# Reordering first operands, projection steps, a mask and one tile split in an encoder layer

## The chip, the cores and the metric

The kernel runs on one core of a Trainium2 chip. The metric is the device time in microseconds (us) of one execution. Time before: 967.51 us, the median of three runs (967.51, 967.21 and 969.06).

The engines have short names here, as in the profile: PE is TensorE (matmuls), DVE is VectorE, ACT is ScalarE, POOL is GpSimd, SP is SyncE, which issues nearly all DMAs of this kernel. Each engine executes its own instructions in the order of the program; between engines they wait on semaphores.

## The reference

One encoder layer is applied to 256 prompt tokens and to 2048 sample tokens, all in float32, with a width of 1024:

```
h = rms_norm(x, g_pre)
q, k, v, z_a, u_f, z_f = split(h @ w_in)               # w_in is 1024 x 3072
y_a = neighbourhood_attention(q, k, v, rpb)            # 8 heads of 64, 64-column grid,
                                                       # 8 rows x 16 columns window, bias, softmax
y_f = real(fft2(u_f, over tokens and within a group)) @ w_f + b_f
mixed = [rms_norm(y_a, g_na) * silu(z_a), rms_norm(y_f, g_f) * silu(z_f)]
out = x + rms_norm(mixed @ w_out, g_post)
```

## The kernel before

**Numbers.** Every float32 matrix product is done as three matmuls in a reduced format (`mm3`, L159 to L162: high by high, low by high, high by low). For this each operand x is split: `h` is a copy of x on ACT, rounded to the format, and `l = x - h` is a subtraction, mostly on DVE. So a split is a pair of an ACT instruction and a DVE instruction behind it, and PE needs `h` first and `l` one matmul later.

**Stages, in order of time.** (1) Projections v and u of the prompt and the other four prompt projections: the loop `for b in range(16)`, up to about 119 us. (2) `vu(0, ...)`, v and u of the sample's second product family, 14 groups of 12 matmuls, 119 to 158 us. (3) The projection steps `for i in range(16)` with seven groups `j` each, with `vu(1, ...)` between steps 7 and 8, up to about 530 us. (4) The Fourier stages. (5) The attention loop `for k in range(2, 37)`, four head pairs `pr` of nine groups `i` each, with the Fourier half of the output product `f_mm` between. (6) The dense run, the attention half of the output product `a_mm`, from about 869 us.

The order of the instructions is the program's: everything is written out by hand, and an operation stands in its engine's queue where its function is called. Buffers are taken from pools in turn, and the writer of a new tile waits until the readers of the tile that had the buffer are done. The pool `k8` holds tiles of 8 KB per partition: the tokens `nx` and their combinations, the splits `xh`, `xl` of them, and the rows `xm` whose squares are summed for the norm.

**Functions that the change touches.**
- `op_split(j)` (L466) splits operand j of `vu`: per half `vh` on ACT (L477) and `vl` on DVE (L478); for j = 5 in other forms (L473, L474). `op_load` issues the loads (L463).
- `n_first(j)` (L425) makes the token operand j of `vu(0)`: `xh` on ACT (L428) and `xl` on DVE (L429), both from `k8`.
- `rows_load(i)` (L288) loads 256 rows into a tile `xm` of `k8`; `rows_square(i)` (L292) squares them on ACT (L295) with a sum.
- `hooks` and `at(i, ...)`: functions called ahead of the i-th group of `vu`. In `vu(0)` a hook is called behind the `op_load` and `op_split` of the same group. The order of groups is j = 0, 0, 1, 1, 2, 2, 3, 3, 4, 4, 5, 5, 6, 6; the evictions (L505) of a group follow its matmuls.
- `w_load`, `w_sums`, `a_split`: load of the weights of a projection step (L232 by `load`), four POOL sums (L532), and the splits `wa` (ACT L546, DVE L547). They are called one or two steps ahead.
- `u_load`, `u_split` (ACT L367, DVE L368), `u_stage1` (two pairs of matmuls `pz`, copy `z` on ACT L375, store to `ZD`): the first Fourier stage on 16 tiles `ut`, strewn between the groups of the steps 9 to 14.
- `n_load`, `n_scale` (DVE L400), `n_diff` (POOL, with stores `n_put`): the tokens of the second pass, in steps 1 to 4.
- `mask_p(pr)` (POOL L1114): subtracts the prompt's mask from a bias table; `bias_max` (DVE L1207) of the next head pair's first group reads it. `soft` divides the softmax on POOL (L1219).
- `ys_split(d)` (ACT L1440, DVE L1445): splits a tile of the output product; `atiles[1]` is the second one of the dense run. `pv` multiplies probabilities and v (L1543) and finishes a tile of attention (`y`, L1557; `sqa`, L1563).

Of the kernel before, what the change touches and what calls it, by code (L numbers as in the profile page):

```python
# [164 lines left out]
def build(tc, A, O):  # L165
# [590 lines left out]
    for b in range(16):  # L756
        kind, blk = divmod(b, 4)
        if 1 <= b < 10:
            wz_load(1)
        if b == 2:  # L760
            n_load((1, 1))
        if b in (5, 7):
            r_put(b // 2 + 1)
        if b == 10:
            op_load(0)
        if b == 12:
            op_load(1)
        if 2 <= b < 14:
            b_raw(b + 2)
        if 2 <= b < 8:  # L770
            x, y = divmod(b, 2)
            n_scale(None, *divmod(x, 2)[::-1], range(2 * y, 2 * y + 2))
        elif 8 <= b < 12:
            n_sum(b - 8)
        if b in (5, 12, 13):
            n_first((5, 12, 13).index(b) + 1)
        if b > 13:
            op_split(b - 14)
        p = mmt(512)[:, :TP]
        wh, wl = wb.pop(b)  # L780
        for k in range(KC):
            mm3(nc, p, wh[:, k], wl[:, k], hp_[:, k], lp_[:, k], k == 0, k == KC - 1)
        o = st.tile([128, 256], F32, tag="f", name="f", bufs=3)
        if kind % 2:
            i, d = p, o
        else:
            i = p.rearrange("p (b r c) -> p b r c", b=2, c=32)
            d = o.rearrange("p (r b c) -> p b r c", b=2, c=32)
        nc.scalar.activation(d, i, AF.Silu if kind < 2 else AF.Copy)
        if kind < 2:  # L790
            nc.sync.dma_start(zD[kind, blk * 128:blk * 128 + 128, :TP], o)
        else:
            nc.sync.dma_start((kD if kind == 2 else qD)[blk, :, :TP], o)
# [15 lines left out]
        hooks.setdefault(i, []).append(call(f, *a))  # L809

    for x in range(4, 7):
        at(3 * x - 12, n_first, x)
    for x in range(4):
        at(2 * x + 1, rows_load, x + 5)
        at(2 * x + 4, rows_square, x + 5)
# [19 lines left out]
    for i in range(16):  # L835
        sg, pr = divmod(i, 8)
        if i == 8:
            hooks.clear()
            for x in (5, 6):
                at(2 * x - 9, b_split, x)  # L840
            for x in range(4):
                if x:
                    at(4 * x, wo_load, x)
                at(4 * x + 5, wo_split, x)
            at(20, w_load, 8)
            at(24, w_sums, 8)
            for j in range(7):
                at(24 + j // 2, a_split, 8, j)
            vu(1, range(4), hooks)
        kind, blk = divmod(2 * pair(i), 4)  # L850
        o = [st.tile([128, 1024], F32, tag="f", name="f", bufs=3) for x in range(2)]
        uu = {}

        def e_(name):
            uu[name] = st.tile([128, 512], F32, tag="e", name=name, bufs=6)
            return uu[name]

        def dst(f, b):
            if kind % 2 == 0:
                return o[f].rearrange("p (x b c) -> p b x c", b=2, c=32)[:, b]  # L860
            if kind == 1:
                return o[f].rearrange("p (a b j) -> p b a j", b=2, j=256)[:, b]
            return o[f].rearrange("p (y b x c) -> p y x b c", y=2, b=2, c=16)[:, b]

        def src(a):
            if kind % 2 == 0:
                return a.rearrange("p (x c) -> p x c", c=32)
            if kind == 1:
                return a.rearrange("p (a j) -> p a j", j=256)
            return a.rearrange("p (x b c) -> p x b c", b=2, c=16)  # L870

        def comb(f, b, u, p, op=ALU.add):
            nc.vector.tensor_tensor(out=dst(f, b), in0=src(uu[u]), in1=src(p), op=op)  # L873

        def store(f):
            ts = slice(TP + 1024 * sg, TP + 1024 * sg + 1024)
            if kind < 2:
                silu_[0] = nc.scalar.activation(o[f], o[f], AF.Silu)
                nc.sync.dma_start(zD[kind, (blk + f) * 128:(blk + f) * 128 + 128, ts], o[f])
            else:  # L880
                nc.sync.dma_start((kD if kind == 2 else qD)[blk + f, :, ts], o[f])

        silu_ = [None]
        for j in range(7):
            if i in (0, 8):
                if j in (0, 3):
                    w_load(i + 1 + j // 3)
                if i == 0 and j == 0:
                    a_split(0, 6)
                if i == 0 and j == 1:  # L890
                    row_scales(10, 8)
                if i == 0 and j == 4:
                    iv_rows(10, 8)
                    iv_put(10, 8)
                if i == 0 and j == 6:
                    iv_get(10, 8)
                if j == 2:
                    w_sums(i + 1)
                for x in {3: (0, 1), 4: (2, 3), 5: (4, 5), 6: (6,)}.get(j, ()):
                    a_split(i + 1, x)  # L900
            elif i not in (7, 15):
                if j == 0:
                    w_sums(i + 1)
                a_split(i + 1, j)
                if j == 3 and i < 14 and i != 6:
                    w_load(i + 2)
            elif i == 7:
                if j in (3, 4):
                    op_load(j - 3)
                if j in (5, 6):  # L910
                    op_split(j - 5)
                if j == 5:
                    wo_load(0)
            if sg == 0:
                x, y = divmod(7 * (pr - 1) + j, 14)
                if x in (0, 1):
                    if y == 0:
                        n_load(x)
                    elif 3 <= y < 7:
                        n_scale(x, *divmod(y - 3, 2))  # L920
                    elif 7 <= y < 12:
                        n_diff(x, y - 7)
                if pr == 6 and j in (2, 5):
                    (b_split if j > 2 else b_get)(0)
                if pr == 7 and j:
                    b_get(j)
                    if j > 2:
                        b_split(j - 2)
            if i == 2 and j == 0:
                for t, n in ((gmix, "gmix"), (bfs, "bf"), (dnyq, "dnyq"), (rmask, "rmask"), (csm, "csmask")):  # L930
                    nc.sync.dma_start(t, A[n])
                nc.sync.dma_start(cm, A["cmask"].rearrange("p (b x) -> p b x", b=2))
            for f, d in ((u_load, 0), (u_split, 4), (u_stage1, 6)):
                x = 7 * pr + j - 7 - d
                if sg and 0 <= x < 38 and x % 7 in (2, 4, 6):
                    f(x // 7 * 3 + x % 7 // 2 - 1)
            if i == 5 or 8 <= i < 15:
                t_step(max(0, i - 7), j)
            if i == 15 and j in (1, 3, 4, 5):
                if j == 1:  # L940
                    d2 = [load_d(0), load_d(1)]
                else:
                    zgs.append(load_z(j - 3))
            if 9 <= i < 15 and j == 2:
                v_copy(i - 9)
            p = mmt(512)
            aw = aop[i, j]
            bh, bl = bnew[sg, j]
            for k in range(4):
                mm3(nc, p, aw[:, 0, k], aw[:, 1, k], bh[:, k], bl[:, k], k == 0, k == 3)  # L950
            add = lambda o, u: nc.vector.tensor_tensor(out=e_(o), in0=uu[u], in1=p, op=ALU.add)
            if j == 0:
                nc.scalar.copy(e_("u0"), p)
            elif j == 1:
                comb(0, 0, "u0", p)
            elif j == 2:
                add("u2", "u0")
            elif j == 3:
                add("u4", "u2")
            elif j == 4:  # L960
                comb(1, 1, "u4", p)
                add("u3", "u2")
            elif j == 5:
                comb(1, 0, "u3", p, ALU.subtract)
                store(1)
            else:
                comb(0, 1, "u4", p)
                store(0)
        if kind < 2:
            silu = silu_[0]  # L970
# [624 lines left out]
    for k in range(2, len(G) + 1):  # L1595
# [48 lines left out]
        if g:  # L1644
            if k + 1 < len(G):
                split_q(G[k + 1])
            soft(g, 1)
            if k == 2:
                ys_mul(ftiles[x])
# [6 lines left out]
            f_mm(k, range(6, 12))  # L1656
        else:
            a_mm(atiles[0], 1, range(6))
        if pr < 3 and i == 8:
            mask_p(pr + 1)  # L1660
        if k % 2 and x < 18:
            ys_split(ftiles[x])
        if pr < 3 and i in (5, 6, 7, 8):
# [2 lines left out]
            ys_split(atiles[0])  # L1666
        if g:
            f_evac(k)
        if f:
            pv(f)  # L1670
        if k + 1 in NT:
# [15 lines left out]
        if k in (34, 35):  # L1687
            ys_load(atiles[k - 33])
            of_load(atiles[k - 34])
        if k == 36:  # L1690
            ys_split(atiles[1])


    def evac(d, p, ns, q):
# [110 lines left out]
```

## Time and profile before

| | |
|---|---|
| Median of three runs | 967.51 us (967.21 to 969.06) |
| The profiled execution | 968.71 us, of which 966.9 us are the span |
| PE busy | 957.0 us, 99% |
| DVE, ACT, POOL busy | 710.4, 496.2, 429.8 us |
| Granted PE clock, mean | 0.997 |
| DMA moved | 269.81 MB, mean 279 GB/s |

How to read the lines below: a row of the timeline has the start in us from the span's start, the duration in us, the engine, the line of the kernel, the operation, output<-input by tile names, the shapes (partitions x elements), the count (several rows on end of one kind are put together) and in brackets the idle time of the engine before it with what ended that. The waits view has engine, instruction, releaser, then total us, times, longest. The profiled execution is 1.2 us above the median of the runs.

### The profile page before, as it was taken

The page shows a single profiled execution, that of the slowest core. Times are in us where ns is not written, and L with a number is a line of the kernel's source. Part 1 is how long each engine was busy: PE and PEld are TensorE (multiplying, and loading weights), DVE is VectorE, ACT ScalarE, POOL GpSimd, SP SyncE. Part 2 cuts the span into 40 slices and gives each one's busy share as a digit, 9 for nine tenths or more (in the row PEclk, how much of TensorE's full clock was granted, in tenths as well). Part 3 has the DMA queues.
Part 4 walks back from the last instruction along what each step waited for, and adds up shares of the span by engine and source line. Part 5 has one row for each costly group of instructions (what it writes and reads, how often), then busy time and mean ns, then how long its engine had stood idle before and what let it go on. Part 6 is the DMA issues. An engine that isn't in the chain of part 4 may idle for free.

```text
span 966.9 us, 16988 instructions
## 1 busy us (share of the span) xinstructions
PE 957.0 (99%) x5743; PEld 798.7 (83%) x5743; DVE 710.4 (73%) x1310; ACT 496.2 (51%) x1077; POOL 429.8 (44%) x400
## 2 busy tenths in 40 slices
PE   9999999999999999999999999999999999999997
PEld 8889988888888888888887889787787887778886
DVE  6758978687886855798887358776666656649997
ACT  5845676423335432233344267676676766644443
POOL 2200002455752202665655044567677786524544
PEclk9999999999999999999999999999999999999998
DMA  8899696557748893599888895698877998979993
GB/s 304 323 359 374 243 347 244 194 189 276 292 189 358 293 352 117 193 386 335 294 308 319 292 346 208 197 278 280 267 234 245 273 312 260 281 255 333 342 341 130
DMA packets 140942, 269.81 MB, mean 279 GB/s; under 512 B 13402, under 2 KB 81840, under 8 KB 137464
## 3 DMA queue, kind: packets, MB, share of 16 engines
q1 hardware_dynamic: 140360, 268.32, 79.9%
q8 instruction: 46, 0.75, 0.3%
q10 hardware_dynamic: 432, 0.39, 0.1%
q14 instruction: 40, 0.33, 0.1%
q0 software_dynamic: 64, 0.02, 0.0%
HBM read 179.00 MB, written 96.81 MB: 285 GB/s over the span
## 4 chain that ended last, share of the span: by engine, by line
PE 92%; DMA 3%; DVE 1%; SPq 1%; ACT 1%; issue 1%; POOL 1%; DVEq 0%; ACTq 0%; POOLq 0%
PE po L1454 18%; PE mm L161 18%; PE mm L160 17%; PE mm L162 17%; PE pv L1543 5%; PE ptb L1527 5%; PE s L1185 4%; PE pab L1022 2%; DMA wr<-wz 1%; PE py L160 1%; PE py L162 1%; PE py L161 1%; DMA za<-zD 1%; DMA gpre<-gpre 0%; SPq L1153 0%
## 5 line engine op out<-in xcount | busy, mean ns | idle before, releaser
L160 PE MATMUL mm<-xh,wa 128*128 128x512 f32 x448 | 174.4, 389 | 0.0
L162 PE MATMUL mm<-xh,wa 128*128 128x512 f32 x448 | 174.3, 389 | 0.0
L161 PE MATMUL mm<-xl,wa 128*128 128x512 f32 x448 | 174.3, 389 | 0.0
L532 POOL TENSOR_TENSOR ws<-wr 128x512 f32<-128x512 f32 x16 | 23.3, 1455 | 219.9 <-DMA wr<-wz 207.1
L1219 POOL TENSOR_SCALAR w<-w,m 128x465 f32<-128x465 f32 (+9 forms) x136 | 85.2, 638 | 44.0 <-DVE m L1216 33.8
L160 PEld LDWEIGHTS mm<-xh,wa 128*128 128x128 f32 x448 | 84.1, 188 | 17.6
L162 PEld LDWEIGHTS mm<-xh,wa 128*128 128x128 f32 x448 | 84.1, 188 | 17.6
L161 PEld LDWEIGHTS mm<-xl,wa 128*128 128x128 f32 x448 | 84.1, 188 | 17.3
L547 DVE TENSOR_TENSOR wa<-wr,wa 128x512 fp32r<-128x512 f32 x60 | 73.1, 1228 | 26.0 <-ACT wa L546 25.9
L1454 PE MATMUL po<-wo,yh 128*128 128x512 f32 x272 | 90.5, 414 | 0.0
L1212 ACT ACTIVATE w<-w,m 128x465 f32<-128x465 f32 (+9 forms) x136 | 78.3, 579 | 17.0 <-DVE m L1207 16.9
L1454 PE MATMUL po<-w,yh 128*128 128x512 f32 x280 | 86.8, 391 | 0.0
L1207 DVE CUSTOM_DVE_ANT_1 w<-s,tb 128x465 f32<-128x465 f32 (+8 forms) x124 | 61.2, 531 | 10.9 <-PE s L1185 10.4
L161 PE MATMUL mm<-vl,xh 128*128 128x512 f32 x168 | 65.5, 390 | 0.2 <-DVE vl L478 0.2
L160 PE MATMUL mm<-vh,xh 128*128 128x512 f32 x168 | 65.4, 389 | 0.0
L162 PE MATMUL mm<-vh,xl 128*128 128x512 f32 x168 | 65.4, 389 | 0.0
L585 POOL TENSOR_TENSOR mt<-mt,rmask 128x880 f32<-128x880 f32 (+2 forms) x24 | 50.3, 2110 | 31.6 <-DVE mt L581 25.1
L873 DVE TENSOR_TENSOR f<-u,mm 128x512 f32<-128x512 f32 x64 | 43.4, 678 | 27.1 <-PE mm L162 22.4
L1454 PEld LDWEIGHTS po<-w,yh 128*128 128x128 f32 x280 | 52.1, 188 | 11.2 <-issue 0.4
L546 ACT CAST wa<-wr 128x512 fp32r<-128x512 f32 x60 | 36.4, 617 | 44.5 <-PE mm L162 22.8
L1527 PE MATMUL ptb<-ident,w 128*120 128x128 f32 (+8 forms) x422 | 58.9, 276 | 0.1
L1543 PEld LDWEIGHTS pv<-pt,v 120*64 120x64 f32 (+9 forms) x880 | 47.5, 136 | 13.9 <-issue 9.9
(265 smaller groups left out, 2390.0 us busy)
## 6 DMA issues: line engine op xcount, KB each, us to landing
wr<-wz SPq DMA_DIRECT2D x48, 512.0 KB
vl<-sD SPq DMA_DIRECT2D x20, 512.0 KB
xm<-xm SPq DMA_DIRECT2D x9, 1024.0 KB
oD<-ofs SPq DMA_DIRECT2D x18, 512.0 KB
of<-oD SPq DMA_DIRECT2D x18, 512.0 KB
yr<-yD SPq DMA_DIRECT2D x34, 256.0 KB
zD<-f SPq DMA_DIRECT2D x16, 512.0 KB
xD<-nx SPq DMA_DIRECT2D x14, 512.0 KB
```

The costliest lines, as they stand in the source:

```text
L160: nc.tensor.matmul(out, lh, rh, start=first, stop=False)
L161: nc.tensor.matmul(out, lh, rl, start=False, stop=False)
L162: nc.tensor.matmul(out, ll, rh, start=False, stop=last)
L547: nc.vector.tensor_tensor(out=o[:, 1], in0=src, in1=o[:, 0].bitcast(F32), op=ALU.subtract)
L585: nc.gpsimd.tensor_tensor(out=o, in0=i, in1=rmask[:, m0:m0 + n].unsqueeze(2).to_broadcast([128, n, 80]), op=ALU.add)
L873: nc.vector.tensor_tensor(out=dst(f, b), in0=src(uu[u]), in1=src(p), op=op)
L1207: nc.vector.tensor_tensor_reduce(out=rows(g["w"][b][:, h, :n], w), in0=rows(g["s"][2 * b + h][:, :nr * sw(w)], sw(w))[:, :, :w], in1=tv, s ...
L1212: nc.scalar.activation(w, w, AF.Exp, bias=m[:, h:h + 1], scale=-1.0, accum_out=m[:, 2 + h:3 + h])
L1219: nc.gpsimd.tensor_scalar(w, w, m[:, 4 + h:5 + h], 1.0, ALU.mult, ALU.mult)
L1454: nc.tensor.matmul(p, (d["l"] if x == 2 else d["h"])[:, c], w(n, int(x == 1), c), start=j == 0, stop=j == 11)
L1527: nc.tensor.transpose(ptb[h][:nk, j * 128:j * 128 + 128], g["w"][b][:, h, c0:c0 + nk], ident)
L1543: nc.tensor.matmul(p[hs, b], g["v"][:nk, v, hs], g["pt"][b][:nk, h, j * 128:j * 128 + 128], start=j == 0, stop=j == len(ch) - 1)
```

## The change

Five moves; no instruction is added or removed, and the order of PE's instructions stays.

1. In the loop over b, `op_split(0)` is called at b = 13 instead of 14, and `n_first(3)` at b = 14 instead of 13.
2. In `vu(0)`, `n_first(6)` is called at hook 8 instead of 6; `n_first(4)` and `n_first(5)` stay at 0 and 3.
3. In the projection steps, the u-tile functions and the token functions are called at the start of a group, ahead of `w_load`, `w_sums` and `a_split`, instead of behind them.
4. In the attention loop, `mask_p` is called ahead of `soft(g, 1)` instead of behind the second half of `f_mm`.
5. At k = 36, `ys_split(atiles[1])` is called ahead of `pv(f)` instead of at the end of the step.

```diff
-        if b in (5, 12, 13):
-            n_first((5, 12, 13).index(b) + 1)
-        if b > 13:
-            op_split(b - 14)
+        if b in (5, 12, 14):
+            n_first((5, 12, 14).index(b) + 1)
+        if b in (13, 15):
+            op_split((b - 13) // 2)
...
     for x in range(4, 7):
-        at(3 * x - 12, n_first, x)
+        at((0, 3, 8)[x - 4], n_first, x)
     for x in range(4):
         at(2 * x + 1, rows_load, x + 5)
         at(2 * x + 4, rows_square, x + 5)
...
         for j in range(7):
+            for f, d in ((u_load, 0), (u_split, 4), (u_stage1, 6)):
+                x = 7 * pr + j - 7 - d
+                if sg and 0 <= x < 38 and x % 7 in (2, 4, 6):
+                    f(x // 7 * 3 + x % 7 // 2 - 1)
+            x, y = divmod(7 * (pr - 1) + j, 14)
+            if sg == 0 and x in (0, 1):
+                if y == 0:
+                    n_load(x)
+                elif 3 <= y < 7:
+                    n_scale(x, *divmod(y - 3, 2))
+                elif 7 <= y < 12:
+                    n_diff(x, y - 7)
             if i in (0, 8):
                 if j in (0, 3):
                     w_load(i + 1 + j // 3)
...
-                x, y = divmod(7 * (pr - 1) + j, 14)
-                if x in (0, 1):
-                    if y == 0:
-                        n_load(x)
-                    elif 3 <= y < 7:
-                        n_scale(x, *divmod(y - 3, 2))
-                    elif 7 <= y < 12:
-                        n_diff(x, y - 7)
...
-            for f, d in ((u_load, 0), (u_split, 4), (u_stage1, 6)):
-                x = 7 * pr + j - 7 - d
-                if sg and 0 <= x < 38 and x % 7 in (2, 4, 6):
-                    f(x // 7 * 3 + x % 7 // 2 - 1)
...
+            if pr < 3 and i == 8:
+                mask_p(pr + 1)
             soft(g, 1)
...
-        if pr < 3 and i == 8:
-            mask_p(pr + 1)
...
+        if k == 36:
+            ys_split(atiles[1])
         if f:
             pv(f)
...
-        if k == 36:
-            ys_split(atiles[1])
```

## The prediction

> **What bounds the kernel now.** I read the busy line and the chain first, then the waits of TensorE, then the timeline around each place that the change touches.
>
> ```profile
> PE 957.0 (99%) x5743; PEld 798.7 (83%) x5743; DVE 710.4 (73%) x1310; ACT 496.2 (51%) x1077; POOL 429.8 (44%) x400
> PE 92%; DMA 3%; DVE 1%; SPq 1%; ACT 1%; issue 1%; POOL 1%; DVEq 0%; ACTq 0%; POOLq 0%
> ```
>
> TensorE (PE) carries the chain and is busy for 99% of the span. The change adds and removes no matmul and keeps their order. It can therefore win only where PE stands still, and lose only where it makes PE stand still. In full flow PE starts one 128x512 matmul each 0.23 us; the two rows at 152.32 and 152.55, quoted further down, show that step. A stall is a longer step between starts. The waits view names two of those concerned:
>
> ```profile
> PE pz L161 <- DVE ut L368: 0.4, 1, 0.4
> PE mm L161 <- DVE vl L478: 0.2, 1, 0.2
> ```
>
> Columns: total us, times, longest. The view counts less than the starts do, because ends of matmuls are modelled. I price by starts, and add what the row behind a stall is longer than the usual 0.39.
>
> **Part 1: op_split(0) at b=13.** The first matmul of vu(0) that needs a low half waits.
>
> ```profile
> 113.97 2.01 ACT L477 CAST vh<-vr 128x1024 fp32r<-128x1024 f32 x2
> 116.27 2.28 DVE L429 TENSOR_TENSOR xl<-nx,xh 128x2048 fp32r<-128x2048 f32 x1
> 118.47 4.62 DVE L478 TENSOR_TENSOR vl<-vr,vh 128x1024 fp32r<-128x1024 f32 x4
> 119.14 0.39 PE L160 MATMUL mm<-vh,xh 128*128 128x512 f32 x1
> 119.74 0.50 PE L161 MATMUL mm<-vl,xh 128*128 128x512 f32 x1 [0.21 <-DVE vl L478]
> ```
>
> The step is 0.60 instead of 0.23, and the row 0.50 instead of 0.39: 0.48 us. VectorE (DVE) runs the 2.28 us xl of n_first(3) ahead of the vl that PE waits for. In the new order the pair of vl comes first; its vh is done at 115.98 by the first row, so vl runs from 116.27 to about 118.6, ahead of 119.08. Nothing new is late: n_first(3) serves a later j, and the second vl pair keeps its place. Gain 0.48.
>
> **Part 2: u tiles and tokens ahead of the weight split.** One place shows on PE.
>
> ```profile
> 508.84 0.62 ACT L367 CAST ut<-ut 128x512 fp32r<-128x512 f32 x1
> 508.75 1.30 POOL L532 TENSOR_TENSOR ws<-wr 128x512 f32<-128x512 f32 x1 [2.55 <-DMA wr<-wz]
> 494.28 0.69 DVE L368 TENSOR_TENSOR ut<-ut 128x512 fp32r<-128x512 f32 x1
> 508.97 1.62 DVE L547 TENSOR_TENSOR wa<-wr,wa 128x512 fp32r<-128x512 f32 x1 [1.63 <-ACT wa L546]
> 510.51 1.77 DVE L368 TENSOR_TENSOR ut<-ut 128x512 fp32r<-128x512 f32 x1
> 511.51 0.39 PE L160 MATMUL pz<-ut,f1h 128*128 128x512 f32 x1
> 512.34 0.50 PE L161 MATMUL pz<-ut,f1h 128*128 128x512 f32 x1 [0.44 <-DVE ut L368]
> ```
>
> The step is 0.83 instead of 0.23, plus 0.11 in the row: 0.71 us. The low half of ut comes behind wa, and beside GpSimd's (POOL's) L532 it takes 1.77 instead of 0.69. Ahead of wa its ACT cast comes at about 508.3 (it changes places with a 0.60 cast), the DVE part at about 509.0, and even at 1.77 us it is done by 510.8, before 511.74. The wa pushed back by one operation is for the next step and has most of a step in hand. The token loads and scalings of the first pass (n_load, n_scale, n_diff) move in the same way; no PE row there shows a wait, and what comes later behind them (a weight load on SP's queue, the z copies, wa) serves the next step: 0, bounded by 0.7 either way from the ut stall. Gain 0.71.
>
> **Part 3: mask_p ahead of soft.** At k=9, 18 and 27 DVE's L1207 waits for the new mask on POOL, and the transposes of w on PE come late.
>
> ```profile
> 727.95 1.55 POOL L1114 TENSOR_TENSOR tb<-cm,tb 128x640 f32<-128x640 f32 x1
> 729.53 0.32 DVE L1207 CUSTOM_DVE_ANT_0 w<-s,tb 128x160 f32<-128x160 f32 x1 [1.23 <-POOL tb L1114]
> 730.46 0.40 PE L1454 MATMUL po<-wo,yl 128*128 128x512 f32 x1
> 730.93 0.83 PE L1527 MATMUL ptb<-ident,w 128*96 128x128 f32 x6
> ```
>
> This is k=18: the step is 0.47 instead of 0.23, so 0.24. At k=9 and k=27 it lies between 0 and 0.24 by the same wait; the starts of PE there are close to flow, so I take 0.06 for both. Put ahead, the mask runs before POOL's two w of this step and pushes them back by 1.55 us. Gain 0.30; if those w become late instead, it is 0 to -0.3.
>
> **Part 4: the dense run's second tile.** At k=36 the split of atiles[1] goes ahead of pv.
>
> ```profile
> 863.79 0.38 ACT L1563 ACTIVATE sqa<-pv 128x256 f32<-128x256 f32 x1 [3.17 <-DVE y L1557]
> 863.27 0.42 DVE L1557 TENSOR_TENSOR y<-pv,za 128x256 f32<-128x256 f32 x1 [1.84 <-PE pv L1543]
> 864.42 0.40 PE L1454 MATMUL po<-w,yl 128*128 128x512 f32 x1
> 864.74 0.73 PE L1454 MATMUL po<-w,yh 128*128 128x512 f32 x2
> 865.60 0.50 PE L1454 MATMUL po<-w,yl 128*128 128x512 f32 x1
> 865.94 0.64 PE L1454 MATMUL po<-w,yh 128*128 128x512 f32 x2
> 956.72 0.75 DVE L1696 SCALAR_TENSOR_TENSOR of<-po,inva,of 128x512 f32<-128x512 f32 x1 [1.22 <-PE po L1454]
> ```
>
> From 864.42 to 865.94 PE starts four matmuls in 1.52 us; at 0.23 they take 0.91, so 0.61 is lost to yh and yl, which ACT and DVE make only behind pv's sqa and y. Both engines had been idle ahead of these, ACT for 3.17 us and DVE for 1.84: there yh and yl fit, and they are ready before 864. The dense run that follows is close on DVE as well, but the last row shows DVE waiting 1.22 us for PE at its end: PE is still the later by more than 0.61, so the gain reaches the end. Gain 0.61.
>
> Gains together: 0.48 + 0.71 + 0.30 + 0.61 = 2.10 us.
>
> **Part 5: n_first(6) at hook 8 instead of 6 of vu(0), the loss.** This is more than a shift by two groups. The xl of n_first takes a buffer of the pool k8 which a token-row tile xm holds, and waits for the square that reads it last:
>
> ```profile
> 142.19 2.29 DVE L429 TENSOR_TENSOR xl<-nx,xh 128x2048 fp32r<-128x2048 f32 x1 [2.67 <-ACT xm L295]
> 147.87 0.68 DVE L505 TENSOR_TENSOR vuo<-u,mm 128x512 f32<-128x512 f32 x1
> 150.26 2.35 DVE L478 TENSOR_TENSOR vl<-vl,vh 128x1024 fp32r<-128x1024 f32 x2
> 138.17 1.90 ACT L428 CAST xh<-nx 128x2048 fp32r<-128x2048 f32 x1
> 139.98 1.05 ACT L295 ACTIVATE xm<-xm 128x1024 f32<-128x1024 f32 x1
> 142.07 1.99 ACT L473 ACTIVATE vh<-vl 128x1024 fp32r<-128x1024 f32 x2
> 145.48 1.06 ACT L295 ACTIVATE xm<-xm 128x1024 f32<-128x1024 f32 x1 [1.43 <-DMA xm<-xm]
> 152.32 0.39 PE L160 MATMUL mm<-vh,xh 128*128 128x512 f32 x1
> 152.55 0.39 PE L161 MATMUL mm<-vl,xh 128*128 128x512 f32 x1
> 153.67 1.54 POOL L532 TENSOR_TENSOR ws<-wr 128x512 f32<-128x512 f32 x1 [123.31 <-DMA wr<-wz]
> 153.37 2.39 DVE L547 TENSOR_TENSOR wa<-wr,wa 128x512 fp32r<-128x512 f32 x2 [0.16 <-ACT wa L546]
> ```
>
> At hook 6 it was the square of rows_load(6), whose pair starts at 139.98: xl 2.21 later, at 142.19. At hook 8 the next free buffer is that of rows_load(7), whose square waits for its load until 145.48. Queued behind the waiting xl on DVE are four evictions L505 and the vl pair of op_split(6), which the last group of PE, j=6, needs. Step by step: ACT does the squares of rows_load(6) at 139.98 or a little before, then vh of op_split(5) at 142.07 as now, and xh behind it at 143.97 (I take 1.90 for the pair of 1.99, since rows on one engine overlap by some 0.1); xh keeps ACT until 145.78 (1.81, as from 138.17 to 139.98); the squares go from 145.78, xl starts at 145.78 + 2.21 = 147.99 and keeps DVE 2.21 (142.19 to 144.40, where the next row starts); four L505 take 150.26 - 147.87 = 2.39; the first vl starts at 152.59 and ends 1.21 later at 153.80. PE, earlier by part 1, wants it at 152.55 - 0.48 = 152.07 and gets it at about 153.85: a stall of 1.78 us.
>
> The second vl is wanted six matmuls on, at 153.85 + 1.36 = 155.21. Alone it is ready at 154.95: nothing more. But POOL's first L532 arrives at 153.67, while the first vl runs. The last row is the nearest case: POOL came in while the first of two L547 ran, had its turn ahead of the second, and the pair took 2.39 where two of 0.69 take 1.38. Then POOL runs from 153.80 to about 155.0, the second vl ends at 156.1, and PE loses 156.1 - 155.21 = 0.88 us more. POOL's arrival lies 0.13 us before the point that decides it, less than this sum can resolve, so I take half: 0.44 (ends 0 and 0.88). Loss 1.78 + 0.44 = 2.2 us, between 1.8 and 2.7. The first weights of the projections, behind it, are pushed back with PE.
>
> **The sum.** 2.2 - 2.1 = +0.1. The profiled execution took 968.71 us, 1.8 more than its span of 966.9 and 1.2 more than the median of 967.51; by this sum it would take 968.8, and against the median it gives **967.6 us**: no change that a measurement can tell (0.2% is 1.93 us).
>
> **Rivals.** *A, the new wait doesn't bite* (0.2): xl takes another buffer or its square is done by 146.2, 1.8 us sooner than I put it. Then the gains stand alone: 967.51 - 2.10 = 965.4. For it: a DVE wait of 2.67 us of the same kind was hidden before. Against it: the square's wait of 1.43 us for its load at 145.48, which the change doesn't shorten.
>
> *B, slower* (0.1): the load of rows_load(7) lands over 1.1 us later. In the new order the load of rows_load(8) no longer waits for xl and is issued some 5 us sooner, while that of rows_load(7) is still on its way. If the two share the engines, xl slips, the first vl begins behind 153.67, and both vl wait for a POOL operation in turn: first vl at 156.1, second at 158.3, a loss of 4.0 + 0.9 = 4.9, and 967.51 + 4.9 - 2.1 = 970.3; with 2.5 us of delay it is 971.8. Against it: the loads that SP issued within 134.91 to 136.5 landed in the order of issue:
>
> ```profile
> 134.91 0.40 SPq L290 DMA_DIRECT2D xm<-xm  x1
> 135.41 1.11 SPq L463 DMA_DIRECT2D vl<-sD  x2
> ```
>
> the xm was there at 145.48, and the two vl behind it were split only from 147.58 on. The Trainium skill, "DMA: Bandwidth & Descriptors", section "Queues, rings and completion order", says that a later descriptor may finish before an earlier one and that completion is not first in, first out for an issuing engine; by that rule B would be the likely case and the sum +2.8. No run here shows such an overtaking, so B keeps 0.1.
>
> *C, the gains are hidden* (0.05): each stall is replaced by one behind it, and only the loss is left: 967.51 + 2.2 = 969.7. The 1.22 us at 956.72 speak against it for part 4.
>
> **How the numbers follow.** The forecast has 0.65, from 967.2 to 968.1 by the ends of the loss, and 0.5 more each way for run-to-run spread (the three runs lie 967.2 to 969.1). The range goes from A's 965.4 less 0.2 to below C: 965.2 to 969.3. Faster by over 0.2% is below 965.6: over half of A and a few hundredths of the forecast, 0.14. Slower, above 969.4: B and most of C, 0.13. The rest, 0.73, is no change.
>
> **What would show it.** In the new trace: PE at 119 and 511 steps by 0.23; the transposes at 730 and the matmuls at 865 too; a new row L161 waiting for vl L478 near 153 with 1.5 to 2 us between starts; DVE's xl near 148 waiting for ACT xm. I am wrong if that xl starts before 146.2, if PE shows no stall in 151 to 156, or if a stall of over 0.5 us stands at a place not named here.

## The result

The changed kernel takes 970.04 us (median of nine runs, 969.04 to 972.37); the kernel before takes 967.51 beside it (nine runs, 967.14 to 969.06). The ratio is 1.0030, with a 95% interval of 1.0019 to 1.0041: slower by 2.5 us, where 967.6 was forecast and 969.3 was the upper end. The profiled execution of the changed kernel took 972.37 us, the longest of its runs; that of the kernel before, 968.71, was above its median too.

The first lines of the changed kernel's page:

```profile
span 970.6 us, 16997 instructions
PE 956.3 (99%) x5743; PEld 799.5 (82%) x5743; DVE 699.0 (72%) x1310; ACT 497.3 (51%) x1077; POOL 430.7 (44%) x400
```

Its waits view for TensorE (total us, times, longest) names three large stalls. One of them was forecast, at L478.

```profile
PE mm L161 <- DVE vl L478: 3.4, 2, 2.8
PE py L160 <- DVE Y L1294: 1.7, 1, 1.7
PE mm L160 <- ACT u L953: 1.1, 1, 1.1
```

PE's order is the same in every kernel here, so the start of one and the same matmul can be compared between two traces. This table gives how much later (or sooner, negative) PE is than in the trace of before, in us, at matmuls that start there at the times in the head. It is worked out from the starts of PE's rows in each trace; the kernels are those of the experiments below.

| | 107 | 142 | 188 | 278 | 505 | 551 | 596 | 735 | 804 | 851 | 929 |
|---|---|---|---|---|---|---|---|---|---|---|---|
| after | 0.0 | 0.1 | 4.0 | 5.4 | 5.4 | 4.7 | 6.7 | 6.4 | 6.4 | 4.3 | 3.7 |
| a_hook6 | -0.5 | -1.0 | 0.6 | 5.4 | 5.4 | 4.6 | 5.7 | 5.3 | 5.3 | 3.6 | 3.0 |
| a_notok | 0.4 | -0.1 | 1.6 | 1.6 | 1.6 | 0.9 | 1.2 | 0.9 | 0.9 | -0.8 | -1.4 |
| a_both | -0.5 | -1.0 | -0.4 | -0.4 | -0.4 | -1.2 | -0.5 | -0.8 | -0.8 | -1.7 | -2.4 |
| b_hook8 | -0.1 | -0.1 | 1.7 | 1.7 | 1.7 | 1.3 | 1.8 | 2.2 | 2.1 | 0.1 | 0.0 |
| b_tok | -0.1 | -0.1 | -0.1 | 3.7 | 3.7 | 3.0 | 2.8 | 2.8 | 2.8 | 2.4 | 2.4 |
| b_first | -0.3 | -0.8 | -0.2 | -0.2 | -0.2 | -0.2 | 0.2 | 0.3 | 0.3 | -1.8 | -1.8 |
| b_h8_buf | -0.4 | -0.3 | -0.2 | -0.2 | 0.0 | -0.2 | -0.1 | -0.1 | -0.1 | -2.1 | -2.2 |
| b_gain | 0.5 | 0.5 | 0.5 | 0.5 | 0.5 | -0.2 | -0.1 | -0.4 | -0.4 | -2.4 | -3.1 |
| a_h6_wl | -0.4 | -0.9 | -0.3 | 2.5 | 3.1 | 2.4 | 2.4 | 2.1 | 2.1 | 0.1 | -0.6 |
| a_h6_nd | 1.0 | 1.0 | 0.9 | 1.2 | 1.2 | 0.4 | 0.6 | 0.3 | 0.3 | -1.8 | -2.4 |
| a_best | -0.1 | -0.1 | 1.1 | 2.2 | 2.2 | 1.5 | 2.2 | 1.9 | 1.9 | 0.3 | -0.3 |

Three things in it belong to no move. The drop between 804 and 851 of 1.6 to 2.1 us stands in every row but two (a_both has 0.9, b_tok 0.3), also in those that leave that stage alone: the one profiled execution of before had stalls there that others do not have, which fits its being 1.2 us above its median. The first column differs by up to half a us (1.0 in a_h6_nd) through waits in the first 30 us, ahead of every move. And the wait for Y near 590 us (L1294 behind the split of `wo`, which waits for its load) is 2.0 us between 551 and 596 in the trace of the changed kernel, and between -0.2 and 1.0 in the others; no move reaches it, and its share of the difference is left open.

The forecast stall, in the timeline of the changed kernel:

```profile
141.50 1.06 ACT L295 ACTIVATE xm<-xm 128x1024 f32<-128x1024 f32 x1 [1.46 <-DMA xm<-xm]
147.48 1.05 ACT L295 ACTIVATE xm<-xm 128x1024 f32<-128x1024 f32 x1
149.70 2.29 DVE L429 TENSOR_TENSOR xl<-nx,xh 128x2048 fp32r<-128x2048 f32 x1 [2.66 <-ACT xm L295]
154.30 3.45 DVE L478 TENSOR_TENSOR vl<-vl,vh 128x1024 fp32r<-128x1024 f32 x2
154.95 1.71 POOL L532 TENSOR_TENSOR ws<-wr 128x512 f32<-128x512 f32 x1 [124.92 <-DMA wr<-wz]
152.37 0.39 PE L160 MATMUL mm<-vh,xh 128*128 128x512 f32 x1
155.58 0.50 PE L161 MATMUL mm<-vl,xh 128*128 128x512 f32 x1 [2.82 <-DVE vl L478]
156.84 0.40 PE L160 MATMUL mm<-vh,xh 128*128 128x512 f32 x1
157.81 0.50 PE L161 MATMUL mm<-vl,xh 128*128 128x512 f32 x1 [0.57 <-DVE vl L478]
```

The chain is the forecast one: square, xl, four evictions, vl, and POOL's turn between the two vl (the pair takes 3.45 instead of 2.35). In this execution it runs 1.7 us later than forecast (xl at 149.70, not 147.99). The load that is late is that of rows_load(6): ACT waits for it until 141.50 (139.06 in a_notok below, whose program is the same up to here), and what stands behind that square in ACT's queue, the square of rows_load(7) at 147.48 too, follows without a wait. The two steps of 3.21 and 0.97 instead of 0.23, with 0.11 for each long row behind the step, cost 3.9.

The stall that was not forecast, in the timelines of the changed kernel and, for the same instructions, of before:

```profile
248.16 14.20 SPq L404 DMA_DIRECT2D xD<-nx  x6
262.41 1.25 SPq L232 DMA_DIRECT2D wr<-wz  x2
268.14 0.63 ACT L549 ACTIVATE wa<-wr 128x512 fp32r<-128x512 f32 x1 [11.17 <-DMA wr<-wz]
268.67 0.57 ACT L953 COPY u<-mm 128x512 f32<-128x512 f32 x1
267.80 0.39 PE L162 MATMUL mm<-xh,wa 128*128 128x512 f32 x1
269.29 0.50 PE L160 MATMUL mm<-xh,wa 128*128 128x512 f32 x1 [1.10 <-ACT u L953]
```

```profile
243.79 9.19 SPq L404 DMA_DIRECT2D xD<-nx  x5
253.07 1.20 SPq L232 DMA_DIRECT2D wr<-wz  x2
257.97 0.64 ACT L549 ACTIVATE wa<-wr 128x512 fp32r<-128x512 f32 x1 [6.89 <-DMA wr<-wz]
258.51 0.57 ACT L953 COPY u<-mm 128x512 f32<-128x512 f32 x1
264.00 0.39 PE L160 MATMUL mm<-xh,wa 128*128 128x512 f32 x1
```

Before, SP issues five token stores and then the weight load of step 6; after, six. The sixth waits for one more combination on POOL, and the load is issued at 262.41 instead of 253.07; PE itself is 4.0 us late here. ACT's first split of step 6 waits for it, and behind it in ACT's queue stands the copy `u` that PE needs. In before ACT sat idle for the same load too, 6.89 us, but PE did not wait: the copy was done at 259.08 (258.51 + 0.57), and the matmul that needs it started in flow at 264.00. So 4.9 us were in hand. In the changed kernel the split comes 10.2 us later (268.14 against 257.97), which is 6.1 more than PE's lateness: 1.2 us more than there was in hand, and PE's step is longer by 1.3.

The three stage gains are there. At 516.94 the matmuls of `pz` step by 0.23; at k=18 the step to the transposes is 0.23; and at the second tile yl runs at 865.66, ahead of y, with PE in flow:

```profile
516.94 0.39 PE L160 MATMUL pz<-ut,f1h 128*128 128x512 f32 x1
517.17 0.39 PE L161 MATMUL pz<-ut,f1h 128*128 128x512 f32 x1
737.05 0.39 PE L1454 MATMUL po<-wo,yl 128*128 128x512 f32 x1
737.28 0.82 PE L1527 MATMUL ptb<-ident,w 128*96 128x128 f32 x6
865.66 0.69 DVE L1445 TENSOR_TENSOR yl<-yr,yh 128x512 fp32r<-128x512 f32 x1
867.58 0.42 DVE L1557 TENSOR_TENSOR y<-pv,za 128x256 f32<-128x256 f32 x1 [1.23 <-PE pv L1543]
```

### The profile page after: what moved, and what is told of

Read it like the earlier page. It is cut to its first block, busy times and chain, and to the rows that moved or that the text cites. A ratio compares the mean times of both kernels' runs of the same rounds, so it can differ in the third digit from the quotient of the medians.

```text
span 970.6 us, 16997 instructions
## 1 busy us (share of the span) xinstructions
PE 956.3 (99%) x5743; PEld 799.5 (82%) x5743; DVE 699.0 (72%) x1310; ACT 497.3 (51%) x1077; POOL 430.7 (44%) x400
## 4 chain that ended last, share of the span: by engine, by line
PE 91%; DMA 4%; DVE 2%; issue 1%; POOL 1%; ACT 0%; SPq 0%; DVEq 0%; POOLq 0%; ACTq 0%
PE po L1454 20%; PE mm L160 16%; PE mm L161 16%; PE mm L162 16%; PE pv L1543 6%; PE ptb L1527 6%; PE s L1185 4%; PE pab L1022 2%; DMA wr<-wz 2%; DMA vN<-vuo 1%; DMA wr<-wo 1%; DMA vl<-sD 1%; DVE vl L478 1%; PE py L160 1%; PE idle L225 1%
## 5 line engine op out<-in xcount | busy, mean ns | idle before, releaser
L547 DVE TENSOR_TENSOR wa<-wr,wa 128x512 fp32r<-128x512 f32 x60 | 69.5, 1165 | 21.2 <-ACT wa L546 21.1
L1207 DVE CUSTOM_DVE_ANT_1 w<-s,tb 128x465 f32<-128x465 f32 (+8 forms) x124 | 61.2, 532 | 10.2 <-PE s L1185 9.6
L1531 DVE COPY pt<-ptb 120x384 f32<-120x384 f32 (+5 forms) x72 | 40.5, 563 | 27.7 <-PE ptb L1527 27.5
```

Of the source, the lines that this page charges most:

```text
L547: nc.vector.tensor_tensor(out=o[:, 1], in0=src, in1=o[:, 0].bitcast(F32), op=ALU.subtract)
L1207: nc.vector.tensor_tensor_reduce(out=rows(g["w"][b][:, h, :n], w), in0=rows(g["s"][2 * b + h][:, :nr * sw(w)], sw(w))[:, :, :w], in1=tv, s ...
```

## The experiments

Each ran beside the kernel before on the same chip; the medians of before were 967.56, 967.1, 967.23 and 967.43 in the four groups. Runs of one kernel mostly spread over 3 to 5 us, so a ratio tells about 1 us; the traces tell the rest.

**a_hook6: the changed kernel without the move to hook 8.**

```diff
-        at((0, 3, 8)[x - 4], n_first, x)
+        at(3 * x - 12, n_first, x)
```

> The changed kernel with n_first(6) back at hook 6, the other four moves kept. Theory 1 (the new wait of VectorE in vu(0) costs what the trace of the changed kernel shows, about 4.0 us on TensorE at 152 to 158 us): that stall is gone and the median falls from 970.0 to about 966. Theory 2 (the wait costs what the prediction said, 2.2 us, and the rest of that stall is a late stretch of loads that comes with other moves or with the run): about 967.8, with loads that still land 1 us later. Rival (the wait is hidden and the loss lies elsewhere): 970, no change.

Measured: 971.8 us (five runs), ratio 1.0044 (1.0030 to 1.0058). Not faster but, if anything, slower than the changed kernel. The rival's 970 is nearest, but not for its reason: the stall at 153 was real, and it is gone. PE now waits longer at the weights of step 6, and runs slowly behind that wait:

```profile
264.40 0.39 PE L162 MATMUL mm<-xh,wa 128*128 128x512 f32 x1
267.63 0.50 PE L160 MATMUL mm<-xh,wa 128*128 128x512 f32 x1 [2.84 <-ACT u L953]
268.26 0.63 PE L162 MATMUL mm<-xh,wa 128*128 128x512 f32 x1
core 0: us, PE busy (x) PEld busy (x) DVE busy (x) ACT busy (x) POOL busy (x), PEclk, DMA share, GB/s
268.12:271.51 3.39, 3.39 (x10) 2.61 (x9) 2.13 (x3) 0.74 (x2) 3.31 (x3) 0.50 1.04 420
```

The last two lines are a view of one stretch of time; PEclk is the granted PE clock. From 268.1 to 271.5 it is 0.50 instead of 1.00, and PE starts a matmul each 0.43 us (the next ones begin at 268.68 and 269.11) instead of each 0.23. So this kernel is 0.6 late at 188, loses 3.0 in the wait and 1.7 behind it. The changed kernel is 4.0 late at 188, loses 1.3 in the wait and, with its clock at 1.00, 0.1 behind it. That both are 5.4 late at 278 is a coincidence of two things. PE comes to the wait 3.4 us sooner here, but the load is issued only 1.8 us sooner (260.62 against 262.41), so the wait is longer; and the slow stretch comes on top. The five runs have mean granted clocks of 0.995 to 0.997, those of before beside them 0.997 to 0.999, which fits such a stretch in the other runs too. What brings it on is not shown: of all traces here only this one and that of b_tok have one between the start and the end of the kernel, and the step of 3.21 us at 152 in the changed kernel is not followed by one.

This trace also waits for the vl of op_split(5) at 147 (1.6 us lost between 142 and 188, where a_both loses 0.5).

**a_notok: the changed kernel with the token functions back behind the split.**

```diff
-            x, y = divmod(7 * (pr - 1) + j, 14)
-            if sg == 0 and x in (0, 1):
...
             if sg == 0:
+                x, y = divmod(7 * (pr - 1) + j, 14)
+                if x in (0, 1):
...
```

> The changed kernel with the token functions (n_load, n_scale, n_diff) back behind the weight split, the u tiles still ahead. Theory 1 (the stores of n_diff, which wait for GpSimd, now stand in SyncE's queue ahead of the weight load of step 6, so the split of step 6 waits on ScalarE and holds up the copy of u behind it; 1.4 us at 268 us): that stall is gone and the median is about 968.6. Rival (the stall at 268 us is only the shift of 4 us by the first stall meeting a load at a fixed time): it stays, 970.

Measured: 968.04 us, ratio 1.0006 (0.9997 to 1.0015), 2.0 us less than the changed kernel. The wait for u has gone from the view; what is left of the rows above is vl:

```profile
PE mm L161 <- DVE vl L478: 1.2, 2, 0.6
```

Theory 1 holds: the tokens' place makes that stall. In this trace, with earlier loads, the hook-8 stall is 1.7 us (between 142 and 188 in the table), in two steps of 0.96.

**a_both: both moves taken back.**

> The changed kernel with both taken back: n_first(6) at hook 6 and the token functions behind the weight split. What is left is op_split(0) at b=13, the u tiles ahead, the mask and the second tile. Theory 1 (the four gains of the prediction are real): 967.5 - 2.1 = 965.4. Rival (the gains are absorbed further on, by the stalls at 816 to 834 us or by the dense run): 966.5 to 967.5.

Its edit is that of a_hook6 and that of a_notok together. Measured: 966.86 us, ratio 0.9994 (0.9983 to 1.0005). This lies in the rival's range, the interval leaves theory 1's 965.4 out, and the result is not to be told from no change. The trace shows the gains all the same, and one of them given back at a place that the rival didn't name. In it 0.5 us is won at 119 and lost at 146 (the columns 142 and 188), 0.7 is won at 511, 0.3 at the mask and 0.6 at the second tile.

**b_hook8: the kernel before with the move to hook 8 alone.**

> The kernel before with n_first(6) at hook 8 alone. Theory 1 (4.0 us at vu(0)'s last group, less 0.5 because TensorE comes there later without the first move): 967.5 + 3.5 = 971. Theory 2 (the size of the prediction): 967.5 + 1.3 to 2.2 = 969 to 969.7. Rival (hidden): 967.5.

The edit is that of a_hook6, turned round and made in the kernel before. Measured: 969.33 us, ratio 1.0018 (1.0009 to 1.0027), 1.8 us slower. Theory 2 holds for the size, theory 1 with its 4 us falls: the rest was the late load of that one execution.

```profile
147.33 2.29 DVE L429 TENSOR_TENSOR xl<-nx,xh 128x2048 fp32r<-128x2048 f32 x1 [2.66 <-ACT xm L295]
151.93 3.44 DVE L478 TENSOR_TENSOR vl<-vl,vh 128x1024 fp32r<-128x1024 f32 x2
152.59 1.70 POOL L532 TENSOR_TENSOR ws<-wr 128x512 f32<-128x512 f32 x1 [123.30 <-DMA wr<-wz]
152.20 0.39 PE L160 MATMUL mm<-vh,xh 128*128 128x512 f32 x1
153.20 0.50 PE L161 MATMUL mm<-vl,xh 128*128 128x512 f32 x1 [0.61 <-DVE vl L478]
155.43 0.50 PE L161 MATMUL mm<-vl,xh 128*128 128x512 f32 x1 [0.55 <-DVE vl L478]
```

**b_h8_buf: hook 8, but another buffer.**

```diff
-        at(3 * x - 12, n_first, x)
+        at((0, 3, 8)[x - 4], n_first, x)
...
-        at(2 * x + 1, rows_load, x + 5)
+        at((1, 3, 5, 9)[x], rows_load, x + 5)
```

> The kernel before with n_first(6) at hook 8, and rows_load(8) called at hook 9 instead of 7, so that xl takes the buffer of rows_load(6) as before while ScalarE and VectorE keep the order of the hook-8 kernel instruction for instruction. The weights of step 0 are then issued ahead of that load. Theory 1 (it is the buffer: xl waits for the square of rows_load(7)): xl starts near 145.5 us on ScalarE's xh instead of 147.3, the vl pair follows 1.8 us sooner, and both stalls at 152 to 155 us are gone: 967.5. Rival (the place in the order alone, xh behind the vh of op_split(5), or GpSimd's turn between the two vl, makes vl late): stalls of 0.8 us or more stay there, 968.4 to 969.3.

Measured: 967.31 us, ratio 0.9998 (0.9989 to 1.0007). ACT and DVE have the order of b_hook8, instruction for instruction; only the buffer of xl and the place of the load of rows_load(8) among SP's transfers differ, and the 1.8 us are gone.

```profile
145.36 1.05 ACT L295 ACTIVATE xm<-xm 128x1024 f32<-128x1024 f32 x1
145.48 2.29 DVE L429 TENSOR_TENSOR xl<-nx,xh 128x2048 fp32r<-128x2048 f32 x1 [0.57 <-ACT xh L428]
150.08 3.45 DVE L478 TENSOR_TENSOR vl<-vl,vh 128x1024 fp32r<-128x1024 f32 x2
```

xl now waits for its own xh, 1.85 us sooner. The square of rows_load(7) comes at 145.36, no sooner than in b_hook8 (145.11), so with the old buffer xl would have had to wait for it here too. POOL still has its turn between the two vl (3.45), but that early it costs PE 0.2 us at most (columns 142 and 188). The buffer is the cause, not the place in the order.

**b_tok: the kernel before with the token functions ahead alone.**

> The kernel before with the token functions alone ahead of the weight split. Theory 1 (a store of n_diff, which waits for a GpSimd combination, now stands ahead of the weight loads of steps 4 and 6 in SyncE's queue, and the weights of step 6 come late): a wait of TensorE for the copy u (L953) near 260 us of 1.4 to 4.7 us, and a median of 969 to 972. Rival (this wait needs another of the moves too): no such row, 967.5.

The edit is that of a_notok, turned round and made in the kernel before. Measured: 970.0 us, ratio 1.0033 (1.0021 to 1.0044). Theory 1 holds: this move alone costs as much as the whole change.

```profile
244.98 14.20 SPq L404 DMA_DIRECT2D xD<-nx  x6
259.23 1.25 SPq L232 DMA_DIRECT2D wr<-wz  x2
265.96 0.50 PE L160 MATMUL mm<-xh,wa 128*128 128x512 f32 x1 [1.94 <-ACT u L953]
266.40:269.79 3.39, 3.39 (x10) 2.64 (x9) 2.08 (x3) 0.71 (x3) 3.31 (x3) 0.50 1.04 423
```

PE is on time here, and the load is issued 6.2 us later than before (259.23 against 253.07). The rows of POOL and SP account for 6.1 of that: the combinations begin 1.3 us later (248.66 against 247.40), one more of them is waited for (2.7), a weight sum that ran ahead of them has its turn between two (1.7), and the sixth store is issued too (0.4). With 4.9 us in hand, PE loses 2.1 in the wait. Behind it the granted clock is 0.50 from 266.4 to 269.8, as in a_hook6 (the last line is the same view), and PE loses 1.7 more: 3.8 us in this trace, 2.9 between the medians.

**a_h6_wl: the tokens ahead, but w_load ahead of them** (on top of a_hook6).

```diff
+            if 0 < i < 14 and i not in (6, 7, 8) and j == 3:
+                w_load(i + 2)
             x, y = divmod(7 * (pr - 1) + j, 14)
...
-                if j == 3 and i < 14 and i != 6:
-                    w_load(i + 2)
```

> The changed kernel with n_first(6) back at hook 6, the token functions ahead as changed, but w_load called ahead of them in the same group, so that only its place in SyncE's queue differs from the run of 971.8. Theory 1 (it is the place of w_load behind the stores): the wait at 268 us is gone and the time falls by about 4 us to that of the kernel without both moves, 966.9. Rival (GpSimd's combinations ahead of the last weight sum, or VectorE's scalings ahead of wa, make the weights late): the wait stays, 970 to 972.

Measured: 968.12 us, 1.0 above before beside it, where a_hook6 is 4.2 above; ratio 1.0006 (0.9997 to 1.0016). Theory 1 has most of it: the wait for u falls to 0.3 us, and no stretch at half the clock follows. But the rival keeps a part. The trace still loses 2.9 us between 188 and 278 (a_hook6 4.7), most of it in a wait of another kind at 246:

```profile
246.47 0.47 PE L160 MATMUL mm<-xh,wa 128*128 128x512 f32 x1 [1.71 <-DVE f L873]
```

**a_h6_nd: n_load and n_scale ahead, n_diff with its stores behind** (on top of a_hook6).

```diff
-                elif 7 <= y < 12:
-                    n_diff(x, y - 7)
...
             if sg == 0:
+                x, y = divmod(7 * (pr - 1) + j, 14)
+                if x in (0, 1) and 7 <= y < 12:
+                    n_diff(x, y - 7)
```

> The changed kernel with n_first(6) back at hook 6, n_load and n_scale ahead as changed, n_diff with its stores at its old place behind the weight split. Theory 1 (the stores ahead of w_load): no wait at 268 us, about 966.9. Rival (the scalings on VectorE, which wait for the token loads ahead of wa, start the delay): a wait of over 1 us for wa or u between 180 and 280 us, 968 to 972.

Measured: 967.18 us, ratio 1.0001 (0.9992 to 1.0010). Theory 1 holds: five stores stand ahead of the weight load again, and neither of the two waits is there.

```profile
247.40 9.21 SPq L404 DMA_DIRECT2D xD<-nx  x5
256.70 1.21 SPq L232 DMA_DIRECT2D wr<-wz  x2
```

So of the token functions it is n_diff, its combinations on POOL and its stores on SP, that costs; the loads and scalings cost nothing that the runs can tell, as was forecast for all of them.

**b_first: op_split(0) at b=13 alone.** The edit is the first hunk of the diff.

> The kernel before with op_split(0) at b=13 and n_first(3) at b=14 alone. Theory 1 (the 0.48 us won at 119 us is lost again at 146 us, where the vl of op_split(5) is ready at a time that the loads set and TensorE now comes too early): no wait of L161 at 119, a step of 0.6 to 0.8 instead of 0.23 at 146, the starts of the matmuls behind 158 us no sooner than before, 967.5. Rival (the gain stays): the starts behind 158 us are 0.5 sooner, 967.0.

Measured: 966.98 us, ratio 0.9999 (0.9990 to 1.0008). Theory 1 holds in the trace:

```profile
118.85 0.40 PE L160 MATMUL mm<-vh,xh 128*128 128x512 f32 x1
119.08 0.40 PE L161 MATMUL mm<-vl,xh 128*128 128x512 f32 x1
146.08 0.39 PE L160 MATMUL mm<-vh,xh 128*128 128x512 f32 x1
146.76 0.50 PE L161 MATMUL mm<-vl,xh 128*128 128x512 f32 x1 [0.30 <-DVE vl L474]
```

The step at 119 is 0.23, and PE is 0.48 sooner from there (-0.30 to -0.78 in the table). At 146 it waits 0.45 and 0.11 for the vl of op_split(5), whose time the loads and the square of rows_load(6) set, and is back at -0.21.

**b_gain: the kernel before with the u tiles, the mask and the second tile.**

> The kernel before with three of the five moves: the u tiles ahead, the mask ahead, the second tile's split ahead; no move of op_split(0), of n_first(6) or of the tokens. The prediction's gains for these are 0.71 + 0.30 + 0.61 = 1.62: about 966. Rival (op_split(0) at b=13 is worth its 0.48 too, so this is slower than the kernel with it, 966.9 measured): 967.3.

Measured: 966.54 us, ratio 0.9995 (0.9984 to 1.0006). The trace shows 0.7, 0.3 and 0.6 us at the three places; the median is 0.6 below that of before, and the interval holds both 1.5 us faster and no change. So the sum of these gains is seen in the trace and not settled by the runs.

**a_best: the changed kernel with both causes taken out**, the edits of a_notok and the second hunk of b_h8_buf.

> The changed kernel with the two causes of loss taken out: the token functions behind the weight split as before, and rows_load(8) at hook 9, so that xl of n_first(6) at hook 8 takes a free buffer. Theory 1 (with op_split(5) now ahead of that xl, the 0.48 us of op_split(0) is not lost at 146 us any more, and the four gains add up): TensorE starts 0.5 sooner than before from 158 us on, 1.2 from 520, 1.5 from 740, and the median is 967.3 - 2.1 = 965.2. Rival (a gain is given back at a later wait, as that of op_split(0) was): 966.5, as for three gains.

Measured: 967.75 us, ratio 1.0005 (0.9995 to 1.0015). Neither: it beats nothing. In its trace the load of rows_load(6) is late again (ACT squares from 140.55, and xl starts at 146.66 instead of 145.48), POOL's turn between the two vl costs PE 0.85 us at 154.77, and there is a wait for f at 247 of 0.9 us that no theory had.

```profile
PE mm L160 <- ACT xh L284: 1.0, 1, 1.0
PE mm L160 <- DVE f L873: 0.9, 1, 0.9
PE mm L161 <- DVE vl L478: 0.6, 1, 0.6
```

No version here is clearly faster than the kernel before; the lowest ratios are those of a_both (0.9994) and b_gain (0.9995).

## Why the prediction was wrong

**The step that failed is the price of the token functions in part 2.** It put them at 0, "bounded by 0.7 either way", because no PE row there waited and because "a weight load on SP's queue" that comes later "serves the next step". Alone they cost 2.9 us (970.0 against 967.1), 2.0 in the changed kernel (970.04 against 968.04), and a_hook6 and a_both, measured beside each other, differ by 4.9. Three things were not priced. The load is late by all that the store ahead of it waits for, 6.2 us in b_tok. The time in hand was never counted: that the load is "for the next step" was true, but the split that waits for it holds up, on its engine, a copy that belongs to the step in progress, and the rows of before, ACT at 257.97 and 258.51 and PE at 264.00, show 4.9 us between that copy and its user. And behind the longer waits PE ran at half its clock for 3.4 us, another 1.7 in the traces of b_tok and a_hook6. The bound of 0.7, taken from another stall, bounded nothing.

**Part 5, the loss at hook 8: right in mechanism, a little large in size.** Forecast 2.2, between 1.8 and 2.7; measured 1.8 alone, 1.7 in the trace of a_notok and 1.2 as the difference of a_notok and a_both. The changed kernel's own profiled execution shows 3.9, with a late load. The term that was too large is the first vl: 0.85 us instead of 1.78, since xl starts at 147.3 and not at 147.99. POOL's turn, which I took at half of 0.88, came in full, 0.85. That the buffer is the cause is shown by b_h8_buf.

**Part 1, op_split(0): the gain is real and is given back.** The 0.48 at 119 is in b_first and in a_both, and both lose it at 146 us. "Nothing new is late" was the wrong step: the vl of op_split(5), which I did not look at, was only just in time before. At hook 8 the gain goes into the other stall, as forecast.

**Parts 2 (u tiles), 3 and 4: right on the path.** 0.73, 0.33 and 0.63 in the traces, against 0.71, 0.30 and 0.61; every trace with these moves has them. The last two are in no trace without the moves. The first depends on when PE arrives: between 505 and 551 b_hook8 drops by 0.4 and b_tok by 0.7 without the move, because the stall of before is smaller there or absent.

**The sum.** Forecast: 2.2 lost, 2.1 won. Measured between medians, taking the tokens out first and hook 8 next: tokens 2.0, hook 8 1.2, and all the rest -0.7 (a_both against before, interval -1.6 to 0.5), together +2.5. In the other order the shares are not the same, as the 4.9 above shows. Rival B, a late load of rows_load(7), gave 970.3, close to the 970.04 measured, but by luck: hook 8 alone costs 1.8 and not 4.9, and even in the profiled execution at 972 us the square of rows_load(7) waits for no load. The load that is late there is that of rows_load(6); what it adds in the other executions was not tried.

**The order of loads.** The Trainium skill ("DMA: Bandwidth & Descriptors", section "Queues, rings and completion order") has completion not first in, first out for an issuing engine. In a_notok the load of rows_load(8) is issued at 136.40 instead of 144.51, and that of rows_load(7) still lands first: ACT squares the rows of the latter from 145.06 without a wait, and waits 0.93 us for those of the former until 150.07. The runs give no sign of an overtaking there.

## What to carry to other kernels

Before an operation is put ahead of a load in a queue, look up the load's user and count the time in hand: from the end of what stands behind that user in its engine's queue to the instruction that needs it, whatever step it belongs to. Here that was 4.9 us, and one store that waits for another engine took 6.2. An engine that sits idle for the load is a reason to count, and not yet a loss. Price a wait by the starts of the matmuls behind it too: twice here a wait of 2 to 3 us was followed by 1.7 us lost at half the granted clock. Parts of a change do not add: undoing one loss alone showed nothing here, and a gain of 0.5 us was lost 27 us later. And where a wait comes from a buffer taken in turn, moving the call changes which buffer it gets: check the releaser, not the place.

## What the runs showed that I had not expected

The loads of one stretch shift between executions by more than most terms of the sum. The square of rows_load(6) waited for its load until 141.50 in the trace of the changed kernel and until 139.06 in that of a_notok, whose programs are the same up to there, and the square of rows_load(7) behind it began at 147.48 and at 145.06; that made one stall 3.9 us in the one and 1.7 in the other. Before's own profiled execution had some 2 us between 804 and 851 us that most other traces don't have. And in two traces the granted clock halved for 3.4 us in the middle of the kernel, which no busy share shows: PE counts as busy there. A single profiled execution names the waits, but does not price one that ends on a load.
